# Up stores from ScalarE and GpSimd, rows of the last projection by GpSimd's queue, its sums in the third product, and the combination's gate columns two ahead

## The chip, the cores and the metric

The kernel runs on one core of a Trainium2 chip. The core has five engines that run side by side, each through its own list of instructions in order: TensorE (PE, matrix products), VectorE (DVE), ScalarE (ACT), GpSimd (POOL) and SyncE (SP). An engine that waits for a semaphore holds back all that stands behind in its list. Transfers between the memory outside (HBM) and the on-chip memory are issued by an engine and carried by 16 DMA engines. The metric is the device time of one execution in microseconds (us); the time before is the median of three runs.

## The reference

One decoder layer over 1024 positions of width 1024, in float32. The input x is normalised and projected by w_in into the columns of two branches and two gates. The branches are mixed, and a gated feed-forward network with a short causal convolution follows:

```python
y_a = conformer_branch(u_glu, ...)
y_b = ssd_branch(z, xbc, dt_raw, ...)
mix = (sigmoid(gate_a) * y_a + sigmoid(gate_b) * y_b) @ w_o
h = layer_norm(DN_ALPHA * h + mix, ln1_g, ln1_b)
u = causal_dwconv(h @ w_up, dw_w, dw_b)          # 3 taps, 2 x 2816 columns
gate, val = split(u, 2)
h = layer_norm(DN_ALPHA * h + (silu(gate) * val) @ w_down, ln2_g, ln2_b)
```

## The kernel before, in words

**Numbers in two parts.** Every product is made to float32's precision from three passes: a value is split into a high half (a cast by ScalarE, L731, L1006) and a low half (value less high half, by VectorE, L732, L1007), and `mm3` (L166 to L168) adds high x high, high x low and low x high. A weight tile is thus loaded by a transfer issued by SyncE, cast by ScalarE and subtracted by VectorE before TensorE can use it.

**Stages.** The sequence is handled in two halves of 512 positions up to the mixing; per half the layer norm, the branches (`mixers`), and `combine`. `combine(hh, hT, yT)` makes eight column tiles: for each j a product with the gate weights gb_j over hT, a sigmoid into the tile gb, a product with the branch's output weights sp_j over yT, and sum and product with gb. yT is the transposed state-space branch; its last quarter comes in just ahead of this stage: TensorE transposes it (L192), ScalarE writes the high half (L198), VectorE the low half (L199).

**The up projection** uses a scheme with seven block products instead of eight (Strassen's, in Winograd's form). The weights of a column pair j come as two 512 KB tiles, ra (blocks a11, a12) and rb (a21, a22). For the first LEAD = 8 columns two of the seven products are made early, in `up_first`, while the mixing's last norms are still running; their sums are stored to first_scr (L815, 16 stores of 256 KB) and loaded again in `up_rest` (L859, L860). `up_weights` makes s3 = a11 + a21, a21 + a22 and two more sums in place (L828 to L831) and splits three weights from them: w_s24 (from ra), w_s10 (from rb) and w_s3. Loads of ra take the ring "st" (three buffers, shared with all other weights), loads of rb the ring "raw" (three buffers). `up_rest` runs over j = 0 to 21: the products into the columns ug (gate) and uv (value), then for each the convolution of three taps (L883 on ScalarE, L887 twice on VectorE) into a buffer fo, of which there are three, then silu and the product (L898). An even j gives an early block that is stored at once (L908, b11); an odd j gives b2 (L910) and with it the sums t32 and t41 for the down projection (L912 to L915, stores L916 and L917). The first two columns of ug and uv are zeroed by GpSimd for each j (L846, L847).

**The down projection** (`down`) uses the same scheme with seven products p over 11 steps k. `load(p, k)` loads a block of the stored activations into the right half of a buffer dr and a weight block into its left half, forms the weight's sum where one is needed, and splits both in one go. Product 0 needs a11, product 1 a12, product 2 the sum a22 + a21 + a11, and product 3 the sum a11 + a21 (here called c3), product 6 c4 = a12 + a22 + a11 + a21. Before the change c3[k] is summed in product 0 (a21 loaded to c3[k] by L971, a11 added by L940), c4[k] begun in product 1 (L975) and completed in product 3. The raw buffers of these loads alternate between "st" and "raw". The eight residual rows (512 KB each, L936) are loaded when `down` begins.

**What sets the order.** The program is written by a scheduler that sorts instructions by the place in the code and by the priority of a `tc.high_priority(offset=...)` block; each engine then runs its list in order. All transfers before the change are issued by SyncE, so a transfer that waits for its data holds back every later one. A buffer of a ring is taken again when its last reader has finished, a store's end included.

## Time and profile before

| | |
|---|---|
| times of three runs | 2043.0, 2043.06, 2047.3 us (median 2043.06) |
| profiled execution | 2043.0 us, its span 2043.0 us |
| mean granted TensorE clock | 0.99 |
| busy: TensorE, VectorE, ScalarE, GpSimd | 1977.0, 1717.1, 1001.3, 146.8 us |
| moved | 275.10 MB, 135 GB/s in the mean |
| matmuls in a full window of 50 us | 222 |

In the rows below, the parts of a line of the timeline are its start, its duration, the engine and line number, the operation with output and input names (numbers left out), and in brackets the idle time of the engine ahead of it with what ended it. PE stands for TensorE's matmuls, PEld for its weight loads, SPq for SyncE's issues of transfers. Where TensorE has stood still, the granted clock drops to 0.5 and matmuls are 0.43 us apart instead of 0.23. A matmul's duration (about 0.39 us) is longer than its distance to the next, since they overlap.

### The profile page before, as it was taken

What the parts mean: (1) busy time and instruction counts of PE and PEld (TensorE: products, weight loads), DVE (VectorE), ACT (ScalarE), POOL (GpSimd) and SP (SyncE); (2) the same over time, 40 slices, a digit from 0 to 9 for tenths busy, and PEclk for the clock granted to TensorE, in tenths of its full rate; (3) what the DMA queues carried; (4) which work ended last, traced back from release to release, by engine and by line L of the source; (5) the groups of instructions that cost most, each with busy time, mean ns of one, the idle gap of its engine ahead of it and who ended that gap; (6) DMA issues with size and microseconds to landing.
All of it is one profiled execution on the core that took longest, in us unless ns stands there. A gap on an engine that the chain in (4) does not pass through costs nothing. (4 is left out here: it accounts for less than half of the span.)

```text
span 2043.0 us, 24683 instructions
## 1 busy us (share of the span) xinstructions
PE 1977.0 (97%) x9164; PEld 1627.7 (80%) x9164; DVE 1717.1 (84%) x2279; ACT 1001.3 (49%) x1431; POOL 146.8 (7%) x125
## 2 busy tenths in 40 slices
PE   7999999999999999999999999997899999989998
PEld 6888887888788888888888888876678888768886
DVE  7599999989766859999998976596888788789668
ACT  4465654556452356665454645453334445444432
POOL 2010101000400001010100040010000000000000
PEclk9999999999999999999999999998989999999999
DMA  6212223223436522222323253564343223287463
GB/s 218 93 68 89 87 93 103 98 103 114 160 124 218 200 93 73 93 78 87 117 88 109 107 175 127 207 234 174 124 138 119 95 98 117 101 316 267 145 226 109
DMA packets 99192, 275.10 MB, mean 135 GB/s; under 512 B 11264, under 2 KB 11264, under 8 KB 99072
## 3 DMA queue, kind: packets, MB, share of 16 engines
q1 hardware_dynamic: 99072, 273.52, 38.4%
q8 instruction: 72, 1.18, 0.2%
q14 instruction: 48, 0.39, 0.1%
HBM read 223.93 MB, written 49.55 MB: 134 GB/s over the span
## 5 line engine op out<-in xcount | busy, mean ns | idle before, releaser
L420 DVE SCALAR_TENSOR_TENSOR c<-v,pc,c 128x512 f32<-128x512 f32 x480 | 374.5, 803 | 7.7 <-ACT c L409 6.4
L478 POOL TENSOR_TENSOR au<-seg_mv,head_of 128x1024 fp32r<-128x1024 f32 x32 | 76.4, 2386 | 963.0 <-PE sm L487 730.1
L166 PE MATMUL acc<-hT,w_c 128*128 128x512 f32 x352 | 141.0, 401 | 0.0
L167 PE MATMUL acc<-hT,w_c 128*128 128x512 f32 x352 | 140.6, 399 | 0.0
L168 PE MATMUL acc<-hT,w_c 128*128 128x512 f32 x352 | 138.4, 393 | 0.0
L375 DVE SCALAR_TENSOR_TENSOR xbc<-u,pc,xbc 128x512 f32<-128x512 f32 x144 | 109.6, 773 | 0.7 <-ACT xbc L373 0.5
L1006 ACT CAST w_dn<-dr 128x1024 fp32r<-128x1024 f32 (+1 forms) x73 | 68.3, 944 | 76.6 <-PE sm L168 27.4
L167 PE MATMUL acc<-w_z,hT 128*128 128x512 f32 x256 | 100.8, 394 | 0.0
L166 PE MATMUL acc<-w_z,hT 128*128 128x512 f32 x256 | 100.8, 401 | 0.0
L168 PE MATMUL acc<-w_z,hT 128*128 128x512 f32 x256 | 100.7, 396 | 0.0
L154 ACT CAST w_c<-st_c 128x1024 fp32r<-128x1024 f32 x50 | 52.6, 1051 | 86.9 <-PE acc L168 66.2
L1007 DVE TENSOR_TENSOR w_dn<-dr,w_dn 128x1024 fp32r<-128x1024 f32 (+1 forms) x73 | 78.6, 1086 | 9.3 <-ACT w_dn L1006 9.1
L167 PEld LDWEIGHTS acc<-hT,w_c 128*128 128x128 f32 x352 | 66.1, 188 | 16.9 <-issue 3.8
L168 PEld LDWEIGHTS acc<-hT,w_c 128*128 128x128 f32 x352 | 66.1, 188 | 16.1 <-issue 2.6
L166 PEld LDWEIGHTS acc<-hT,w_c 128*128 128x128 f32 x352 | 66.1, 188 | 16.0 <-issue 2.6
L155 DVE TENSOR_TENSOR w_c<-st_c,w_c 128x1024 fp32r<-128x1024 f32 x47 | 60.5, 1287 | 20.3 <-ACT w_c L154 20.3
L166 PE MATMUL acc<-h1b,w_ue 128*128 128x512 f32 x176 | 68.8, 391 | 2.6 <-ACT w_ue L731 1.4
L731 ACT CAST w_s<-rb 128x1024 fp32r<-128x1024 f32 x22 | 23.2, 1053 | 94.7 <-PE sm L168 73.1
L166 PE MATMUL sm<-h1b,w_s 128*128 128x512 f32 x176 | 69.4, 395 | 0.0
L167 PE MATMUL sm<-h1b,w_s 128*128 128x512 f32 x176 | 69.2, 393 | 0.0
L168 PE MATMUL sm<-h1b,w_s 128*128 128x512 f32 x176 | 69.0, 392 | 0.0
L167 PE MATMUL acc<-h1b,w_ue 128*128 128x512 f32 x176 | 68.5, 389 | 0.0
(348 smaller groups left out, 5859.7 us busy)
## 6 DMA issues: line engine op xcount, KB each, us to landing
st_c<-wcol SPq DMA_DIRECT2D x50, 512.0 KB, 3.5
st_z<-wz SPq DMA_DIRECT2D x32, 512.0 KB, 3.5
dr<-wdown SPq DMA_DIRECT2D x55, 256.0 KB, 4.4
st_wo<-wo SPq DMA_DIRECT2D x24, 512.0 KB, 4.1
ra<-wup SPq DMA_DIRECT2D x22, 512.0 KB, 3.5
rb<-wup SPq DMA_DIRECT2D x22, 512.0 KB, 3.5
t_scr<-fo SPq DMA_DIRECT2D x22, 512.0 KB, 4.3
dr<-t_scr SPq DMA_DIRECT2D x44, 256.0 KB, 3.2
```

What stands on the lines that cost most here:

```text
L154: A.copy(w[:, 0, :], st)
L155: (eng or V).tensor_tensor(out=w[:, 1, :], in0=st, in1=w[:, 0, :].bitcast(F32), op=ALU.subtract)
L166: TE.matmul(ps, wa(0), xa(0), start=start, stop=False, skip_group_check=more)
L167: TE.matmul(ps, wa(0), xa(1), start=False, stop=False, skip_group_check=more)
L168: TE.matmul(ps, wa(1), xa(0), start=False, stop=stop, skip_group_check=more)
L375: V.scalar_tensor_tensor(out=o, in0=u[:, k : k + HALF], scalar=pc[:, wc + k : wc + k + 1], in1=o, op0=ALU.mult, op1=ALU.add,)
L420: V.scalar_tensor_tensor(out=accs[i], in0=v[:, k : k + HALF], scalar=pc[:, wc + k : wc + k + 1], in1=accs[i], op0=ALU.mult, op1=ALU.add,)
L478: G.tensor_tensor(out=au, in0=seg_mv[:, c, :].unsqueeze(1).to_broadcast([P, 8, P]), in1=head_of[:, g, :].unsqueeze(2).to_broadcast([P, 8, P]),
L731: A.copy(w[:, 0, :], src)
L1006: A.copy(w[:, 0, cs], src)
L1007: V.tensor_tensor(out=w[:, 1, cs], in0=src, in1=w[:, 0, cs].bitcast(F32), op=ALU.subtract)
```

## The change

1. In `combine` the product of gate column j is made two columns ahead: gates 0 and 1 stand ahead of the loop, and gate j + 1 is made in pass j from 1 to 6. The ring "gate" has three buffers instead of two.
2. In `up_first` ScalarE issues the 16 stores itself.
3. In `up_weights` the tile rb of column 0 takes a buffer of the ring "st", not of "raw".
4. In `up_rest` ug and uv are three fixed tiles u0 to u2 used in turn, zeroed once; the 44 memsets go. The stores b11, b2, t32 and t41 are issued by GpSimd.
5. In `down` GpSimd issues the loads of the rows; in the code they come after step 2 of products 0 and 2. c3[k] no longer takes a sum in product 0: for k < 5 a second copy of a11 is loaded to c3[k] by GpSimd, for k >= 5 a11 is loaded to c3[k] alone and split from there; a12 goes straight to c4[k] in product 1. Product 2 loads a21 and a22 and makes all three sums; product 3 makes none.

The diff, cut to its core:

```diff
+            def gate(j):
                 pg = bank(1)
                 project(pg, weights(wcol[CT_GB + j], f"gb{hh}_{j}"), hT)
-                gb = pl.tile([P, HALF], F32, tag="gate", bufs=2, name=f"gb{hh}_{j}")
+                gb = pl.tile([P, HALF], F32, tag="gate", bufs=3, name=f"gb{hh}_{j}")
                 A.activation(out=gb, in_=pg, func=AF.Sigmoid)
+                gates[j] = gb
+
+            gate(0)
+            gate(1)
+            for j in range(8):
+                if 0 < j < 7:
+                    gate(j + 1)
+                gb = gates[j]
...
-            SY.dma_start(first_scr[j][q], f)
+            A.dma_start(first_scr[j][q], f)
...
-            r2 = upp.tile([P, D], F32, tag="raw", bufs=3, name=f"rb{j}")
+            if j:
+                r2 = upp.tile([P, D], F32, tag="raw", bufs=3, name=f"rb{j}")
+            else:
+                r2 = wst.tile([P, D], F32, tag="st", name=f"rb{j}")
...
-        ug, uv = (
-            upp.tile([P, T + 32], F32, tag="u", bufs=3, name=f"f{n}{j}") for n in ("ug", "uv")
-        )
+        ug, uv = us[2 * j % 3], us[(2 * j + 1) % 3]
...
-        G.memset(ug[:, :2], 0.0)
-        G.memset(uv[:, :2], 0.0)
...
-            SY.dma_start(b11_scr[j], ov[:, early])
+            G.dma_start(b11_scr[j], ov[:, early])
...
-        SY.dma_start(b2_scr[j - NK], ov)
+        G.dma_start(b2_scr[j - NK], ov)
...
-        SY.dma_start(t32_scr[j - NK], t)
-        SY.dma_start(t41_scr[j - NK], a)
+        G.dma_start(t32_scr[j - NK], t)
+        G.dma_start(t41_scr[j - NK], a)
...
-        for t in range(8):
-            SY.dma_start(rs[t], h1_scr[t * P : (t + 1) * P, :])
+        def load_rows(ts):
+            for t in ts:
+                G.dma_start(rs[t], h1_scr[t * P : (t + 1) * P, :])
...
-                if p == 0:
+                if p == 0 and k < EARLY:
                     SY.dma_start(w_st, a11)
-                    SY.dma_start(c3[k], a21)
-                    add(c3[k], c3[k], w_st)
+                    G.dma_start(c3[k], a11)
+                elif p == 0:
+                    w_st = c3[k]
+                    SY.dma_start(w_st, a11)
                 elif p == 1:
+                    w_st = c4[k]
                     SY.dma_start(w_st, a12)
-                    SY.dma_start(c4[k], a22)
+                elif p == 2:
+                    other = raw("do")[:, E]
+                    SY.dma_start(other, a21)
+                    SY.dma_start(w_st, a22)
+                    add(c3[k], c3[k], other)
+                    add(w_st, w_st, c3[k])
                     add(c4[k], c4[k], w_st)
-                elif p == 2:
-                    SY.dma_start(w_st, a22)
-                    add(w_st, w_st, c3[k])
                 elif p == 3:
                     w_st = c3[k]
-                    add(c4[k], c4[k], c3[k])
...
+                if k == 2 and p in (0, 2):
+                    load_rows(range(2 * p, 2 * p + 4))
```

**How the order moves.** SyncE's list before, from the last stores of `up_first` on; first0_7 is the tile of the first block product of column 7, ra2 and rb0 are weight tiles of columns 2 and 0:

```order
L815 DMA first_scr5_131<-first0_5_11106 128x512
L822 DMA ra2_11414<-wup 128x1024
L815 DMA first_scr5_131<-first1_5_11121 128x512
L815 DMA first_scr6_132<-first0_6_11142 128x512
L815 DMA first_scr6_132<-first1_6_11157 128x512
L815 DMA first_scr7_133<-first0_7_11178 128x512
L815 DMA first_scr7_133<-first1_7_11193 128x512
L824 DMA rb0_11202<-wup 128x1024
L824 DMA rb1_11306<-wup 128x1024
L824 DMA rb2_11416<-wup 128x1024
```

The same place of SyncE's list after the change:

```order
L152 DMA st_ue7_11160<-wup 128x1024
L779 DMA h1_scr_125<-r7_10454 128x1024
L831 DMA ra0_11206<-wup 128x1024
L836 DMA rb0_11208<-wup 128x1024
L831 DMA ra1_11306<-wup 128x1024
L836 DMA rb1_11308<-wup 128x1024
L836 DMA rb2_11414<-wup 128x1024
```

The stores are gone from this list, rb0 stands right behind ra0, and ra2 has gone back behind the loads of columns 0 and 1. ScalarE's list after the change at the end of `up_first` (before, the DMA rows are not there):

```order
L823 COPY first1_6_11157<-acc507_11129 128x512
L823 COPY first0_7_11178<-acc508_11165 128x512
L824 DMA first_scr6_132<-first1_6_11157 128x512
L824 DMA first_scr7_133<-first0_7_11178 128x512
L823 COPY first1_7_11193<-acc508_11165 128x512
L824 DMA first_scr7_133<-first1_7_11193 128x512
L740 CAST w_s3_0_11221<-s3_0_11210 128x512
```

ScalarE now issues the last store between its last copy and the first cast of the up stage, w_s3_0.

VectorE's list before, at the first long gap of the up stage; fo1 and fo23 are the convolution buffers of column 2, fuv3 is the value tile of column 3, s4 the running sum of column 4:

```order
L887 SCALAR_TENSOR_TENSOR fo1_11507<-fug2_11432,pc_107,fo1_11507 128x1024
L887 SCALAR_TENSOR_TENSOR fo23_11511<-fuv2_11433,pc_107,fo23_11511 128x1024
L863 TENSOR_TENSOR s4_11648<-s4_11648,sm523_11655 128x512
L869 TENSOR_TENSOR fuv3_11537<-s3_11538,sm518_11541 128x512
L887 SCALAR_TENSOR_TENSOR fo23_11511<-fuv2_11433,pc_107,fo23_11511 128x1024
```

The same place after the change, where u1 and u2 take the place of fuv3 and fuv2:

```order
L895 SCALAR_TENSOR_TENSOR fo1_11501<-u1_11201,pc_107,fo1_11501 128x1024
L871 TENSOR_TENSOR s4_11636<-s4_11636,sm523_11641 128x512
L895 SCALAR_TENSOR_TENSOR fo23_11505<-u2_11202,pc_107,fo23_11505 128x1024
L877 TENSOR_TENSOR u1_11201<-s3_11530,sm518_11531 128x512
L895 SCALAR_TENSOR_TENSOR fo23_11505<-u2_11202,pc_107,fo23_11505 128x1024
```

The sum on s4 has moved ahead of the first tap of fo23; the sum into u1 (before: fuv3) stands behind that tap in both. One column later, the subtractions L921 and L922 on fo23 and fo12 (before: L913 and L914) stand ahead of the low half of w_s24_6, where before they stood behind it.

SyncE's list before, at the start of the last projection; c3 and c4 are the weight sums, dr the buffers of one step:

```order
L936 DMA rows_13949<-h1_scr_125 128x1024
L968 DMA dr_5_14057<-b11_scr4_138 128x512
L970 DMA dr_5_14057<-wdown 128x512
L975 DMA c4_0_13950<-wdown 128x512
...
L971 DMA c3_13948<-wdown 128x512 x11
L975 DMA c4_6_13956<-wdown 128x512
...
L908 DMA b11_scr10_144<-fo32_13788 128x512
...
L968 DMA dr_7_14097<-b11_scr6_140 128x512
L970 DMA dr_7_14097<-wdown 128x512
```

GpSimd's list after the change, its end (all that SyncE no longer issues there):

```order
L916 DMA b11_scr9_143<-fo31_13450 128x512
L982 DMA c3_13866<-wdown 128x512 x5
L918 DMA b2_scr9_154<-fo42_13577 128x1024
L924 DMA t32_scr9_165<-fo20_13573 128x1024
L925 DMA t41_scr9_176<-fo31_13450 128x1024
L916 DMA b11_scr10_144<-fo32_13710 128x512
L946 DMA rows_13867<-h1_scr_125 128x1024 x8
L918 DMA b2_scr10_155<-fo43_13837 128x1024
L924 DMA t32_scr10_166<-fo21_13833 128x1024
L925 DMA t41_scr10_177<-fo32_13710 128x1024
```

The eleven loads into c3 in a row are gone from SyncE's list (six remain there, each a weight of product 0), and GpSimd issues the other five, then all eight rows loads at one place, between the last b11 store and the last b2, t32 and t41 stores.

More of the change, by code (lines that the diff above doesn't have):

```diff
@@ L590, in combine @@
         with pool(f"comb{hh}") as pl:
-            mb = []
-            for j in range(8):
+            mb, gates = [], {}
+            def gate(j):
                 pg = bank(1)
                 project(pg, weights(wcol[CT_GB + j], f"gb{hh}_{j}"), hT)
-                gb = pl.tile([P, HALF], F32, tag="gate", bufs=2, name=f"gb{hh}_{j}")
+                gb = pl.tile([P, HALF], F32, tag="gate", bufs=3, name=f"gb{hh}_{j}")
                 A.activation(out=gb, in_=pg, func=AF.Sigmoid)
+                gates[j] = gb
[5 more added lines that the diff above has]
+                gb = gates[j]
                 ya = pl.tile([P, HALF], F32, tag="yb", bufs=2, name=f"yb{hh}_{j}")
@@ L646, in combine @@
             for j in range(8):
-                ga = pl.tile([P, HALF], F32, tag="gate", bufs=2, name=f"gl{hh}_{j}")
+                ga = pl.tile([P, HALF], F32, tag="gate", bufs=3, name=f"gl{hh}_{j}")
                 SY.dma_start(ga, g_scr[hh][j])
@@ L835, in up_weights, with up_rest @@
         return ue, w24, w10, w3
-    def up_rest(upp, bl, j, before):
+    def up_rest(upp, us, bl, j, before):
         ue, w24, w10, w3 = up_weights(upp, j)
-        ug, uv = (
-            upp.tile([P, T + 32], F32, tag="u", bufs=3, name=f"f{n}{j}") for n in ("ug", "uv")
-        )
+        ug, uv = us[2 * j % 3], us[(2 * j + 1) % 3]
         s = upp.tile([P, HALF], F32, tag="s", bufs=2, name=f"s{j}")
-        G.memset(ug[:, :2], 0.0)
-        G.memset(uv[:, :2], 0.0)
         early, late = slice(2, 2 + HALF), slice(2 + HALF, 2 + T)
@@ L915, in up_rest @@
         V.tensor_tensor(out=a[:, early], in0=b[:, early], in1=t[:, late], op=ALU.add)
-        SY.dma_start(t32_scr[j - NK], t)
-        SY.dma_start(t41_scr[j - NK], a)
+        G.dma_start(t32_scr[j - NK], t)
+        G.dma_start(t41_scr[j - NK], a)
     def down(upp, dp, g, b):
-        LAST = 8
+        LAST, EARLY = 8, 5
         X, Y = [bank(1) for _ in range(4)], [bank(0) for _ in range(4)]
@@ L1105 @@
     upp = ctx.enter_context(pool("up"))
+    us = [upp.tile([P, T + 32], F32, name=f"u{i}") for i in range(3)]
+    for u in us:
+        G.memset(u[:, :2], 0.0)
     before = None
     for j in range(NF):
-        before = up_rest(upp, bl, j, before)
+        before = up_rest(upp, us, bl, j, before)
     ffn_stack.close()
```

## The prediction

> **What bounds the kernel now.** I read the page first, then the table by windows of 50 us, then TensorE's waits in the windows that fell short, then the chain and the timeline around each wait. The page says who is the bound and which queue carries the transfers:
>
> ```profile
> PE 1977.0 (97%) x9164; PEld 1627.7 (80%) x9164; DVE 1717.1 (84%) x2279; ACT 1001.3 (49%) x1431; POOL 146.8 (7%) x125
> q1 hardware_dynamic: 99072, 273.52, 38.4%
> ```
>
> TensorE is busy for 97% of the span, so a change that leaves its work alone can only win back places where it stands still or runs at a lower clock. GpSimd (POOL) is nearly free. The windows show where TensorE falls short; the columns are start and end, length, then busy time and instructions of each engine, granted clock, DMA share and GB/s:
>
> ```profile
> 500.00:550.00 50.00, 46.32 (x209) 37.59 (x208) 40.34 (x53) 21.91 (x30) 16.36 (x11) 0.97 0.47 158
> 1400.00:1450.00 50.00, 36.77 (x149) 28.89 (x150) 33.78 (x46) 14.49 (x17) 0.20 (x2) 0.90 0.38 137
> 1450.00:1500.00 50.00, 44.83 (x186) 36.35 (x185) 46.03 (x56) 18.14 (x18) 0.60 (x6) 0.93 0.41 137
> 1500.00:1550.00 50.00, 45.50 (x190) 37.07 (x189) 45.21 (x55) 18.76 (x19) 0.60 (x6) 0.93 0.40 143
> 1550.00:1600.00 50.00, 50.00 (x222) 41.41 (x221) 37.79 (x43) 22.93 (x27) 0.40 (x4) 1.00 0.28 100
> 1800.00:1850.00 50.00, 42.36 (x171) 33.46 (x171) 41.52 (x46) 22.18 (x24) 0.10 (x1) 0.93 1.04 386
> ```
>
> A full window holds 222 matmuls, one per 0.225 us. The next to last row is such a window; the three ahead of it lack 73, 36 and 32 matmuls (16.4, 8.1 and 7.2 us), the last lacks 51 (11.5 us), and the first 13 (2.9 us; more in truth, since 16 of its 209 are short transposes). Those 46 us are what this change can work on. TensorE's waits in 1390 to 1560 and in 1790 to 1860 (total, times, longest) name who is late:
>
> ```profile
> PE sm L166 <- DVE fuv L869: 12.3, 3, 5.2
> PE sm L166 <- ACT w_s L731: 10.6, 2, 10.0
> PE acc L166 <- ACT w_dn L1006: 4.4, 1, 4.4
> PE acc L167 <- DVE w_dn L1007: 2.5, 2, 1.3
> ```
>
> **Part 1, gate columns two ahead.** Rows of TensorE in the first combination, with two short windows behind them (TensorE's own busy time is the first number after the length):
>
> ```profile
> 520.97 0.50 PE L166 MATMUL acc<-yT,w_sp 128*128 128x512 f32 x1 [0.83 <-ACT yT L198]
> 524.55 0.50 PE L167 MATMUL acc<-yT,w_sp 128*128 128x512 f32 x1 [2.85 <-DVE yT L199]
> 525.00:527.00 2.00, 2.00 (x8) 1.59 (x7) 0.00 (x0) 0.00 (x0) 0.00 (x0) 0.71 0.92 327
> 527.00:529.00 2.00, 2.00 (x6) 1.56 (x5) 0.00 (x0) 0.43 (x1) 1.49 (x2) 0.50 0.97 306
> ```
>
> TensorE has transposed the last quarter of yT and then waits 0.83 + 2.85 = 3.7 us for its two halves, and the clock then drops for two windows, 2 x 0.29 + 2 x 0.5 = 1.6 us. In the new order twelve matmuls of the third gate column, which need only hT, stand between the transposes and the first use of the new yT: 12 x 0.225 = 2.7 us of cover. About 1 us of the idle time stays, and after so short a gap I expect no drop of the clock: 3.7 - 1.0 + 1.6 = 4.3; I take **-4** (0 to -5.3). The second combination shows no such wait, so it counts nothing.
>
> **Part 2, stores by ScalarE and rb0 in the other ring.** This is the long wait. Rows of several engines, in order of start (the bracket is the idle time before and who ended it):
>
> ```profile
> 1394.40 9.52 SPq L815 DMA_DIRECT2D first_scr<-first  x5
> 1402.99 0.59 ACT L814 COPY first<-acc 128x512 f32<-128x512 f32 x1 [3.15 <-issue]
> 1403.97 1.39 SPq L824 DMA_DIRECT2D rb<-wup  x3
> 1407.89 0.69 DVE L828 TENSOR_TENSOR s<-ra,rb 128x512 f32<-128x512 f32 x1 [14.57 <-DMA rb<-wup]
> 1411.08 0.68 DVE L831 TENSOR_TENSOR ra<-ra 128x512 f32<-128x512 f32 x1
> 1411.80 1.05 ACT L731 CAST w_s<-ra 128x1024 fp32r<-128x1024 f32 x1
> 1412.89 0.80 PE L166 MATMUL sm<-h1s,w_s 128*128 128x512 f32 x1 [9.99 <-ACT w_s L731]
> ```
>
> SyncE holds the three rb loads behind five stores that wait for ScalarE's copies; VectorE starts its sums only when rb0 lands at 1407.9, and TensorE idles 9.99 us. With the stores on ScalarE and rb0 in a "st" buffer, rb0 is issued right behind ra0 and is there long before. What is late next is ScalarE's own order: the cast of s3_0 stands behind the last copy (ends 1403.6) and now behind that copy's store. With one issue at some 0.3 us (the t_scr row below) the cast runs about 1404.0 to 1404.7. VectorE then has four operations ahead of the end of ra0 (low half of s3_0, ra0, s3_1, ra0), 4 x 0.6 to 0.68, so 1407.2 to 1407.4; the cast of ra0 takes 1.05 and TensorE starts near 1408.5 instead of 1412.9: **-4.4**. The other 15 stores cost ScalarE 15 x 0.3 = 5 us in a stage where it is half idle. If ScalarE's issues were dearer (1 us), the gain would be 3.7; if VectorE did the sums without waiting for the cast, 7. The remaining gap of 5.6 us still costs the clock.
>
> **Part 3, stores by GpSimd and tiles u0 to u2.** The chain through the next two long gaps, with the store that starts the second as SyncE's row and TensorE's row at its end:
>
> ```profile
> 1469.14 5.80 DMA t_scr<-fo
> 1475.02 1.16 ACT fo L883
> 1477.46 0.68 DVE s L863
> 1478.14 0.61 DVE fuv L869
> 1504.66 0.32 SPq L916 DMA_DIRECT2D t_scr<-fo  x1
> 1504.66 5.18 DMA t_scr<-fo
> 1509.93 1.16 ACT fo L883
> 1513.70 0.79 PE L166 MATMUL sm<-h1s,w_s 128*128 128x512 f32 x1 [4.50 <-DVE fuv L869]
> ```
>
> A convolution buffer fo is taken again when its store has landed; ScalarE's scaling waits for that, VectorE's taps wait for ScalarE, and in VectorE's queue the sums that let TensorE go on (s, fuv) stand behind the first tap. In the new order only the sum on s4 (0.6 us) moves ahead of that tap; the one that TensorE waits for, now on u1, still stands behind it: **-0.6** at the first gap (5.2 us, the longest of the three in the waits). At the second gap the subtractions ahead of the t32 store are no longer behind the low half of ra6 (1.1 us, by the like operations of the L1007 row in Part 4): **-1.1**. Against this stands the store's issue by GpSimd, once in each gap. No transfer in this trace is issued by GpSimd. Its nearest rows are SyncE's 0.32 us of issue and the 5.18 and 5.80 us to landing; I bound the difference by -1 (the store no longer shares SyncE's queue with loads) and +5 (landing twice as long), and take **+1** each, nearer the lower end because GpSimd is 93% idle and the transfer itself is the same. Together +0.3.
>
> The Trainium skill, page "DMA: Bandwidth & Descriptors", section "Issuing engines are not separate DMA queues", says that another issuing engine saves issue time only; by that rule Part 2's store move would be worth next to nothing. The 9.52 us row speaks otherwise here: what is saved is the wait in order ahead of the loads, not the 0.3 us of an issue. The 44 memsets that go count nothing: none of TensorE's waits above names GpSimd.
>
> **Part 4, the last projection.** Rows of SyncE, TensorE and ScalarE at the change of stage, two windows behind the stall (there of TensorE alone: busy time, clock, DMA share, GB/s), and the page's row of VectorE's low halves (busy us, mean ns of one):
>
> ```profile
> 1813.31 3.59 SPq L975 DMA_DIRECT2D c<-wdown  x6
> 1817.29 7.04 SPq L971 DMA_DIRECT2D c<-wdown  x11
> 1836.69 1.04 ACT L1006 CAST w_dn<-dr 128x1024 fp32r<-128x1024 f32 x1 [7.13 <-DMA dr<-wdown]
> 1837.79 2.07 PE L166 MATMUL acc<-w_dn 128*128 128x512 f32 x4 [4.38 <-ACT w_dn L1006]
> 1837.00:1840.00 3.00, 2.21 (x5) 0.50 1.03 354
> 1840.00:1843.00 3.00, 3.00 (x8) 0.50 1.04 399
> L1007 DVE TENSOR_TENSOR w_dn<-dr,w_dn 128x1024 fp32r<-128x1024 f32 (+1 forms) x73 | 78.6, 1086 | 9.3 <-ACT w_dn L1006 9.1
> ```
>
> The DMA engines are full here (share 1.04 in the window above). SyncE issues 17 c loads in a row, the next dr is late by 7.13 us at ScalarE, and TensorE idles 4.38 us and then runs at half clock to 1843, 5.2 x 0.5 = 2.6 us more. The change halves this demand: products one and two now load 27 + 22 quarter-megabyte pieces instead of 33 + 33. Those 17 x 0.262 MB are 4.5 MB, at 386 GB/s 11.5 us of transfer, against a lateness of 4.4 us at TensorE. The rows (8 x 0.524 MB = 4.2 MB, 10.9 us) leave SyncE's queue ahead of the c loads and come from GpSimd's queue during the first product, so they still share the engines. Net the demand ahead of the stall falls: -4.4 - 2.6 = **-7**. The two waits for VectorE's low half (2.5 us) stand behind the last convolutions, which stay; I leave them. Bounds: 0 if the rows' transfers push dr_9 to dr_11 as late as now, -9.5 if those two waits go as well.
>
> The third product gets three sums per step instead of one, 22 operations of 0.6 us more; VectorE then needs 3 x 0.61 + 1.09 = 2.92 us a step, TensorE 12 x 0.225 = 2.7, so 11 steps fall back 2.4 us. Weight tiles made ahead (six buffers, 16 us) cover this: 0, and +2.4 without the cover.
>
> **Sum.** -4 - 4.4 + 0.3 - 7 = -15.1, on a profiled span of 2043.0 us, equal within 0.1 us to the median of the runs (2043.06): 2027.9.
>
> **Rivals.** *More than the sum:* rb0's early arrival gives VectorE ten microseconds' lead, and the gaps at 1478 and 1513 (5.2 and 4.5 us; with the clock at 0.93 over each window, 0.07 x 50 = 3.5 us behind each) close as well. For it: VectorE is busy 46.0 and 45.2 of 50 in those two windows, near its limit, where a lead counts. Against: the chain there goes through a store's landing, not through VectorE's amount of work. It would add 5.2 + 4.5 + 7 = 16.7 us: 2011.
>
> *Given back:* with VectorE at 92% of the windows, the 4.4 us of Part 2 come back as a longer gap at 1478, and the last projection stays bound by the full DMA engines (share 1.04), since the rows' 4.2 MB now fall into its first steps. Left: Part 1 and little else, 2038.
>
> *Slower, stores that land late from GpSimd's queue:* the fo buffer is freed later. The rows of a quiet column give the slack:
>
> ```profile
> 1569.65 0.32 SPq L917 DMA_DIRECT2D t_scr<-fo  x1
> 1577.05 1.14 ACT L883 ACTIVATE fo<-fuv,pc 128x1024 f32<-128x1024 f32 x1
> ```
>
> 1577.05 - 1569.65 - 5.2 = 2.2 us. A landing later by less than that costs only at the two gaps above. At 5 us later the two gaps pay 10 and seven later pairs 2.8 each, 30 us in all, of which 2 are in the sum: 2028 + 28 = 2056; at 3.5 us, 7 + 9 - 2 = 14, and the gain is used up. It decides from some 3.5 us. The Trainium skill, page "SBUF — State Buffer", section "SBUF: two separate sides" (its box on the trap of VectorE blocking transfers), says that GpSimd writes the descriptors of its transfers itself and is locked out while VectorE runs in a fast two-port mode: a transfer of 620 ns took 3100. No run here shows it yet, and VectorE's operations in this stage (0.68 us for 512 columns of two float32 operands) do not look like a fast mode; hence a small chance.
>
> *The change does not do what it says:* the last stores of the up stage (b2, t32, t41 of the last pair) stand in GpSimd's queue behind the eight rows loads, which wait for buffers and for one another. The second product needs b2 of the last pair in its last step, 13 or more steps of 2.7 us behind the row at 1837.8, so from about 1873. If the store lands later, TensorE waits there: 5 to 8 us back, 2034.
>
> **How the numbers follow.** Chances: forecast 0.60, more 0.12, given back 0.13, late stores 0.09, late queue 0.06. A measurement of this kernel can tell about 0.2%, 4 us, from no change. Faster by more: all of the first two, half of "given back", most of the last: 0.83. Same: the other half and a little of the late stores, 0.09. Slower: 0.08. The range reaches to 2010 for the larger gain and to 2042 for what is given back; outside lie the late stores and the extremes.
>
> **What would show it.** Right: rb0 issued before 1395 and TensorE starting the up columns near 1408 with a gap of 5 to 6 us; matmuls in 500 to 550 at 220 or more; the wait of 4.38 us for w_dn gone and no half clock behind 1837; t_scr stores landing within 6 us of their issue. Wrong: ScalarE waiting longer than now for t_scr, in each pair, or a wait for a dr load in the second product, or a first gap of 9 us or more.

## The result, and the profile after

| | before | changed |
|---|---|---|
| median of 4 runs each, us | 2043.39 | 2034.98 (2030.26 to 2037.27) |
| profiled run, and its span, us | 2043.06, 2043.0 | 2035.35, 2033.6 |

The ratio is 0.9951, with a 95% interval of 0.9937 to 0.9965: faster by 7 to 13 us. The forecast was 2027.9; 8.4 us of the 15.1 forecast came. The page after, engines and DMA queues (packets, MB, share):

```profile
PE 1978.0 (97%) x9164; PEld 1628.0 (80%) x9164; DVE 1710.7 (84%) x2285; ACT 1001.8 (49%) x1448; POOL 171.9 (8%) x141
q1 hardware_dynamic: 87696, 242.06, 35.9%
q0 software_dynamic: 7184, 25.69, 3.3%
q10 hardware_dynamic: 2304, 4.20, 0.6%
```

SyncE's queue is q1; the two new queues, GpSimd's q0 and ScalarE's q10, carry 25.7 and 4.2 MB that it carried before. The same windows as before:

```profile
500.00:550.00 50.00, 48.58 (x227) 39.71 (x226) 40.30 (x54) 22.98 (x31) 15.91 (x11) 1.00 0.48 168
1400.00:1450.00 50.00, 42.86 (x172) 33.70 (x171) 40.00 (x51) 18.98 (x20) 0.73 (x1) 0.93 0.40 135
1450.00:1500.00 50.00, 45.39 (x185) 36.39 (x184) 46.84 (x59) 16.77 (x17) 3.74 (x7) 0.93 0.45 160
1500.00:1550.00 50.00, 48.36 (x212) 39.39 (x211) 47.80 (x57) 22.02 (x24) 2.69 (x5) 1.00 0.35 121
1800.00:1850.00 50.00, 43.18 (x172) 34.53 (x173) 38.16 (x49) 24.03 (x36) 6.40 (x12) 0.90 0.80 295
```

TensorE's counts went from 209, 149, 186, 190, 171 to 227, 172, 185, 212, 172. Three windows gained about 20 matmuls each. The last gained nothing, although its DMA share fell from 1.04 to 0.80: the transfers are fewer and TensorE waits as long. Its waits in 1390 to 1560, then in 1790 to 1860 (total, times, longest):

```profile
PE sm L166 <- DVE u L877: 7.0, 3, 3.9
PE sm L166 <- ACT w_s L740: 6.0, 2, 5.3
...
PE acc L166 <- ACT u L875: 5.4, 1, 5.4
PE acc L166 <- ACT w_dn L1021: 1.8, 1, 1.8
```

The two waits of the up stage fell from 12.3 to 7.0 and from 10.6 to 6.0 us. At the change of stage the wait of 4.4 us for w_dn is down to 1.8, and a new one of 5.4 us stands ahead of it, for a copy of u by ScalarE. Rows around it, of SyncE, GpSimd, ScalarE and TensorE, and a short window of TensorE alone:

```profile
1785.96 3.08 SPq L985 DMA_DIRECT2D c<-wdown  x6
1786.23 2.71 POOL L982 DMA_DIRECT2D c<-wdown  x5 [17.06 <-PE acc L168]
1788.93 0.54 POOL L918 DMA_DIRECT2D b_scr<-fo  x1
1790.21 0.54 POOL L924 DMA_DIRECT2D t_scr<-fo  x1 [0.74 <-issue]
1798.77 1.15 ACT L891 ACTIVATE fo<-u,pc 128x1024 f32<-128x1024 f32 x1 [4.06 <-DMA b_scr<-fo]
1801.51 1.15 ACT L891 ACTIVATE fo<-u,pc 128x1024 f32<-128x1024 f32 x1 [1.59 <-DMA t_scr<-fo]
1804.27 0.79 PE L166 MATMUL acc<-h1s,w_s 128*128 128x512 f32 x1 [5.39 <-ACT u L875]
1811.90 4.25 POOL L946 DMA_DIRECT2D rows<-h_scr  x8 [3.97 <-PE sm L168]
...
1804.00:1808.00 4.00, 3.73 (x9) 0.54 0.01 2
```

Read it from the top. GpSimd's five c3 loads (L982) become free together and run ahead of the next-to-last pair's stores in GpSimd's list. The b2 store follows 2.7 us later, the t32 store behind it. ScalarE can scale into fo only when those stores have landed: it waits 4.06 and 1.59 us, and its copy of u, for which TensorE waits, stands behind both scalings. TensorE idles 5.39 us and restarts at a clock of 0.54: 9 matmuls in 3.73 us where 0.225 us each would give 16.6, another 1.7 us. The clock also falls behind the wait of 1.84 us for w_dn at 1837: it is 0.57 from 1838 to 1841, so that sign of the prediction (no half clock there) did not come.

### The profile page after: what moved, and what is told of

It is laid out like the page before. It is cut to its first block, busy times and chain, and to the rows that moved or that the text cites. A ratio compares the mean times of both kernels' runs of the same rounds, so it can differ in the third digit from the quotient of the medians.

```text
span 2033.6 us, 24571 instructions
## 1 busy us (share of the span) xinstructions
PE 1978.0 (97%) x9164; PEld 1628.0 (80%) x9164; DVE 1710.7 (84%) x2285; ACT 1001.8 (49%) x1448; POOL 171.9 (8%) x141
## 4 chain that ended last, share of the span: by engine, by line
PE 66%; DVE 24%; DMA 4%; issue 4%; ACT 1%; SPq 0%; DVEq 0%; ACTq 0%
PE acc L166 17%; PE acc L168 17%; PE acc L167 17%; DVE c L420 8%; PE sm L166 3%; PE sm L167 3%; PE sm L168 3%; DVE xbc L375 2%; DMA dr<-b_scr 1%; PE acc L357 1%; PE sm L534 1%; DVE fo L895 1%; DMA st_wo<-wo 1%; PE sm L515 1%; DVE w_so L155 1%
## 5 line engine op out<-in xcount | busy, mean ns | idle before, releaser
L166 PE MATMUL acc<-hT,w_c 128*128 128x512 f32 x352 | 141.1, 401 | 0.0
L895 DVE SCALAR_TENSOR_TENSOR fo<-u,pc,fo 128x1024 f32<-128x1024 f32 x88 | 111.5, 1279 | 8.5 <-ACT fo L891 7.8
L166 PE MATMUL acc<-w_z,hT 128*128 128x512 f32 x256 | 100.9, 401 | 0.0
L1021 ACT CAST w_dn<-dr 128x1024 fp32r<-128x1024 f32 (+1 forms) x73 | 60.8, 842 | 77.7 <-DVE dr L951 31.5
L1022 DVE TENSOR_TENSOR w_dn<-dr,w_dn 128x1024 fp32r<-128x1024 f32 (+1 forms) x73 | 69.6, 963 | 17.6 <-ACT w_dn L1021 17.5
L166 PEld LDWEIGHTS acc<-hT,w_c 128*128 128x128 f32 x352 | 66.1, 188 | 15.9 <-issue 2.6
L166 PE MATMUL acc<-h1s,w_s 128*128 128x512 f32 x168 | 66.6, 397 | 5.7 <-ACT u L875 5.7
L166 PE MATMUL acc<-h1b,w_ue 128*128 128x512 f32 x176 | 68.9, 392 | 2.6 <-ACT w_ue L740 1.4
L166 PE MATMUL sm<-h1b,w_s 128*128 128x512 f32 x176 | 70.3, 400 | 0.0
```

What stands on the lines that cost most here:

```text
L166: TE.matmul(ps, wa(0), xa(0), start=start, stop=False, skip_group_check=more)
L895: V.scalar_tensor_tensor(out=o, in0=u[:, k : k + T], scalar=pc[:, wc + k : wc + k + 1], in1=o, op0=ALU.mult, op1=ALU.add,)
L1021: A.copy(w[:, 0, cs], src)
L1022: V.tensor_tensor(out=w[:, 1, cs], in0=src, in1=w[:, 0, cs].bitcast(F32), op=ALU.subtract)
```

## The experiments

The theories. Part 4's gain was lost because the c3 copies in GpSimd's queue delay the stores behind them (the queue theory), or too many bytes come at once at the change of stage, whoever issues them (the bytes theory), or the rows share the engines with the products' loads (the rows theory). For Part 3, which gave more than forecast: VectorE's order moved with the issuing engine (the order theory), or GpSimd's queue lands stores differently (the landing theory). Each ratio is against before on the same chip, where its median was 2044.4 to 2045.6. The change itself was timed beside a before of 2043.39, so a difference between its median and one below carries 1 to 2 us of doubt. "Up" is the distance in the trace from the first product with w_ue to the last, "down" from there to the last with w_dn: before 439.9 and 234.6 us, after 431.8 and 235.4. Among the profiled runs with the change's combination the first product with w_ue starts anywhere from 1348.5 to 1354.1 us, so these distances, and not the totals, carry the verdicts by stage.

**c3 copies by SyncE (e1).**

```diff
-                    G.dma_start(c3[k], a11)
+                    SY.dma_start(c3[k], a11)
```

> The changed kernel, but the five early copies of a11 into c3 are issued by SyncE instead of GpSimd, at the same point. Question: why do the stores of the last odd column but one (b2, t32, t41) land 9.7 to 12.6 us after their issue, so that ScalarE waits for fo and TensorE idles 5.39 us at 1804. Theory A, the DMA engines are full: eleven c3 loads (2.9 MB) start at 1786 and share the 16 engines with the stores; who issues them does not matter. Then the landing stays at 9 us or more, the gap at 4 to 6 us, the time within 2 us of the changed kernel's 2035. Theory B, GpSimd's own list and queue: the stores stand behind the five loads. Then the stores land in 3 to 5 us, the gap falls under 1 us and the time to 2026 to 2029.

Measured: 2026.88 (2024.03 to 2027.84), ratio 0.9905 (0.989 to 0.992), 8.1 us below the change by the medians; up 432.0, down 228.9. GpSimd and TensorE at the same place:

```profile
1785.21 0.53 POOL L918 DMA_DIRECT2D b_scr<-fo  x1 [17.11 <-DVE fo L906]
1798.93 0.50 PE L166 MATMUL acc<-h1s,w_s 128*128 128x512 f32 x1 [1.15 <-ACT u L875]
1831.24 0.50 PE L166 MATMUL acc<-w_dn 128*128 128x512 f32 x1 [1.73 <-ACT w_dn L1021]
```

b2 is stored as soon as its taps are done, and the 5.39 us become 1.15. All eleven c loads still run at once, so bytes alone, whoever issues them, are not what cost those 5 us.

**c3 copies by ScalarE.**

```diff
-                    G.dma_start(c3[k], a11)
+                    A.dma_start(c3[k], a11)
```

> The changed kernel with the five early c3 copies issued by ScalarE, side by side with SyncE's six. GpSimd's list is as in e1, the burst as in the changed kernel: eleven loads from two engines within about 3 us. Theory B (place in GpSimd's list): b2 is issued at once, the stores land as in e1 (7 to 8 us), gap at 1804 of about 1 us, time 2026 to 2028. Theory A', the burst comes too fast (two issuers put 2.9 MB ahead of t32 and t41, one issuer 1.8 MB): the stores land after 9 us or more, gap of 4 to 5 us, time 2033 to 2036. ScalarE itself loses 5 x 0.3 us ahead of two casts, under 1 us for TensorE.

Measured: 2026.81 (2025.68 to 2028.56), ratio 0.9917 (0.99 to 0.9933); down 231.5. The same gain from a third engine: what matters is that the loads leave GpSimd's queue. The issues of 1783 to 1800 (median us to landing) separate its list from its transfers, first after the change, then here:

```profile
c<-wdown SPq DMA_DIRECT2D x6, 256.0 KB, 6.5
c<-wdown POOLq DMA_DIRECT2D x5, 256.0 KB, 7.1
t_scr<-fo POOLq DMA_DIRECT2D x2, 512.0 KB, 11.9
b_scr<-fo POOLq DMA_DIRECT2D x1, 512.0 KB, 9.7
```

```profile
c<-wdown SPq DMA_DIRECT2D x6, 256.0 KB, 8.4
c<-wdown ACTq DMA_DIRECT2D x5, 256.0 KB, 9.7
t_scr<-fo POOLq DMA_DIRECT2D x2, 512.0 KB, 8.3
b_scr<-fo POOLq DMA_DIRECT2D x1, 512.0 KB, 7.6
```

Behind five loads in its own queue, a store takes 9.7 to 11.9 us from issue to landing; with the same loads in another queue 7.6 to 8.3, and the loads are what gets slower. So the stores lost both ways: 2.7 us in the list and 2 to 4 us in the transfers. The amount moved is the same: 4.47 MB in the 14.04 us from the first of these loads after the change, 4.50 MB here. ScalarE pays for it: its five issues took 5.11 us, where 1.5 were expected, TensorE waits 0.90 and 0.53 us for what stands behind them, and the down distance is 2.6 us longer than with the copies by SyncE.

**c3 copies spread out.** Only the first copy stays at the change of stage; the others' a11 are loaded again in the third product.

```diff
-        LAST, EARLY = 8, 5
+        LAST, EARLY = 8, 11
...
-                    G.dma_start(c3[k], a11)
+                    if k == 0:
+                        G.dma_start(c3[k], a11)
...
-                    add(c3[k], c3[k], other)
+                    if 0 < k < EARLY:
+                        first = raw("do")[:, E]
+                        SY.dma_start(first, a11)
+                    else:
+                        first = c3[k]
+                    add(c3[k], first, other)
```

> The changed kernel, but a11 comes through the ring of raw buffers in product 0 for all eleven steps, and a second time through the ring in product 2, where c3 = a11 + a21 is written; only one load goes to c3 early, so that the buffers are handed out as before. The burst at 1786 is 1 load instead of 11; product 2 loads 10 pieces more (4 x 0.262 MB in 2.7 us, 386 GB/s, near what the engines carried in 1800 to 1850). Theory A and theory B: the gap at 1804 goes (5.4 us and about 3 us of clock), stores land in 3 to 5 us; time 2027, up to 2031 if product 2 is starved. Rival C, the stores are late because GpSimd issues them at all: landing stays over 9 us, time 2033 or more.

Measured: 2031.97 (2028.91 to 2035.01), ratio 0.9932 (0.9915 to 0.9949); down 235.8. The gap ahead of the copy of u is 0.84 us, as the queue theory has it, but the loads come back later. TensorE's waits for w_dn from 1790 to the end:

```profile
PE acc L167 <- DVE w_dn L1028: 3.4, 3, 1.9
PE acc L166 <- ACT w_dn L1027: 2.6, 1, 2.6
```

After the change TensorE has no wait behind 1860. Here VectorE is late three times from 1887 to 1897, in the third product. Spreading takes the stall away and pays there.

**The last projection as before.** The whole of down() is undone (rows, c3 copies, sums); Parts 1 to 3 stay.

```diff
-        LAST, EARLY = 8, 5
+        LAST = 8
...
-        def load_rows(ts):
-            for t in ts:
-                G.dma_start(rs[t], h1_scr[t * P : (t + 1) * P, :])
+        for t in range(8):
+            SY.dma_start(rs[t], h1_scr[t * P : (t + 1) * P, :])
...
-                if p == 0 and k < EARLY:
+                if p == 0:
                     SY.dma_start(w_st, a11)
-                    G.dma_start(c3[k], a11)
+                    SY.dma_start(c3[k], a21)
+                    add(c3[k], c3[k], w_st)
...
-                if k == 2 and p in (0, 2):
-                    load_rows(range(2 * p, 2 * p + 4))
```

> The changed kernel with the last projection as it was before (rows and c3, c4 loads by SyncE, sums in products 0, 1 and 3); the up stores stay with GpSimd. The prediction gave this part 7 us: then 2042. The reading of the two traces: from the first to the last matmul of the up and down stages the part gave nothing net (the distance from the last w_ue product to the last w_dn product is 234.6 us before and 235.4 after), because the new gap at 1804 took what the old one at 1837 gave back: then 2033 to 2036, with the gap at 1837 back and none at 1804.

Measured: 2030.56 (2028.29 to 2032.72), ratio 0.9925 (0.991 to 0.994): 4.4 us faster than with Part 4 by the medians, though the intervals of the two ratios just touch. Up 430.0, down 233.8, so 1.6 us of it lie in the down distance. TensorE's waits in 1780 to 1850:

```profile
PE acc L166 <- ACT w_dn L1014: 6.8, 1, 6.8
PE acc L166 <- ACT u L875: 0.7, 1, 0.7
```

The old wait is there in full (6.8 us; 4.4 before) and the new one is not. As written, Part 4 trades one for the other and loses. This run also speaks against the bytes theory: the eight rows loads stand in SyncE's list at the same time, 7.04 MB are moved from 1780 to 1800, and GpSimd's b2 lands after 7.4 us, t32 and t41 after 7.7 (median), with no c3 load ahead of them in their queue.

**Up stores by SyncE (e4).** All 44 stores of b11, b2, t32 and t41.

```diff
-            G.dma_start(b11_scr[j], ov[:, early])
+            SY.dma_start(b11_scr[j], ov[:, early])
...
-        G.dma_start(b2_scr[j - NK], ov)
+        SY.dma_start(b2_scr[j - NK], ov)
...
-        G.dma_start(t32_scr[j - NK], t)
-        G.dma_start(t41_scr[j - NK], a)
+        SY.dma_start(t32_scr[j - NK], t)
+        SY.dma_start(t41_scr[j - NK], a)
```

> The changed kernel with the 44 stores b11, b2, t32 and t41 issued by SyncE again; c3 and rows loads stay with GpSimd. The prediction counted +1 us at each of two gaps for GpSimd's issue and landing: then 2 us less in the up stage, up stage gaps (waits for u, L877) of 5 us instead of 7. Rival: the up stage gained 8.1 us where 4.1 were forecast because the stores left SyncE's list, where loads stood behind them: then 3 to 5 us more in the up stage, gaps of 9 to 12 us as before. For the gap at 1804: theory A keeps it.

Measured: 2034.18 (2032.26 to 2037.09), ratio 0.9942 (0.9923 to 0.996), the same in total and not by stage: up 435.8, 4.0 us longer, down 233.5, 1.9 us shorter. Medians from issue to landing, over 11 stores each: b2 2.9 us by GpSimd and 2.6 by SyncE, t32 3.6 and 3.1, t41 4.8 and 4.0. GpSimd's land 0.3 to 0.8 us later and TensorE's gaps are nevertheless shorter, so the landing theory does not explain the gain. At the change of stage the gap is 5.4 us here too: the b2 store now stands behind SyncE's six c3 loads (issue 1788.39, 2.77 us; the store at 1791.26). That is the queue theory again, in the other list.

**One kind of store each.** b11 and b2 by SyncE, t32 and t41 by GpSimd:

```diff
-            G.dma_start(b11_scr[j], ov[:, early])
+            SY.dma_start(b11_scr[j], ov[:, early])
...
-        G.dma_start(b2_scr[j - NK], ov)
+        SY.dma_start(b2_scr[j - NK], ov)
```

> The changed kernel with the stores b11 and b2 (22) issued by SyncE, t32 and t41 by GpSimd. What made the up stage 4 us shorter with the stores at GpSimd (distance from the first to the last w_ue product: 431.8 us, e4 435.8). Theory L, SyncE's list: b11 and b2 wait longest for VectorE at the head of that list in e4 (33 us in all) and hold the loads behind them: then this kernel has 435 to 436 us and gaps for u of 10 us. Theory O, VectorE's order: with t32 and t41 at GpSimd the scheduler puts the sum on s4 ahead of the first tap of fo23 and the low sum of u2 ahead of fo24's tap, and it does so here too: 432 us, gaps of 7 us.

and t32 and t41 by SyncE, b11 and b2 by GpSimd:

```diff
-        G.dma_start(t32_scr[j - NK], t)
-        G.dma_start(t41_scr[j - NK], a)
+        SY.dma_start(t32_scr[j - NK], t)
+        SY.dma_start(t41_scr[j - NK], a)
```

> The changed kernel with t32 and t41 (22 stores) issued by SyncE, b11 and b2 by GpSimd. VectorE's order in the up stage is that of e4. Theory O: 435 to 436 us from the first to the last w_ue product, gaps for u of 10 us. Theory L: between the two, 432 to 433 us, since the stores that wait longest have left SyncE's list.

Measured: 2032.12 (2031.18 to 2035.2), ratio 0.9936 (0.992 to 0.9952), up 431.0; and 2037.16 (2036.16 to 2039.06), ratio 0.9961 (0.9947 to 0.9975), up 435.1. VectorE ahead of the sum u that TensorE waits for, at the second long gap, with TensorE's row; first with t32 and t41 on GpSimd, then on SyncE:

```profile
1494.05 3.79 DVE L895 SCALAR_TENSOR_TENSOR fo<-u,pc,fo 128x1024 f32<-128x1024 f32 x3
...
1498.96 0.68 DVE L877 TENSOR_TENSOR u<-s,sm 128x512 f32<-128x512 f32 x1
...
1499.70 0.50 PE L166 MATMUL sm<-h1s,w_s 128*128 128x512 f32 x1 [1.70 <-DVE u L877]
```

```profile
1492.81 1.28 DVE L895 SCALAR_TENSOR_TENSOR fo<-u,pc,fo 128x1024 f32<-128x1024 f32 x1
1495.10 2.48 DVE L895 SCALAR_TENSOR_TENSOR fo<-u,pc,fo 128x1024 f32<-128x1024 f32 x2 [1.00 <-ACT fo L891]
...
1498.10 1.28 DVE L895 SCALAR_TENSOR_TENSOR fo<-u,pc,fo 128x1024 f32<-128x1024 f32 x1
...
1499.89 0.68 DVE L877 TENSOR_TENSOR u<-s,sm 128x512 f32<-128x512 f32 x1
...
1500.62 0.50 PE L166 MATMUL sm<-h1s,w_s 128*128 128x512 f32 x1 [4.19 <-DVE u L877]
```

With t32 and t41 on GpSimd three taps stand ahead of u; on SyncE there are four, and one of them waits 1.00 us for a scaling. From the first tap to u that is 4.9 us against 7.1, and TensorE's gap is 1.70 against 4.19. The change itself has the first order (1.64), the kernel with all stores on SyncE the second (3.93). This is what the order theory says. In these four kernels order and queue change together for t32 and t41; the landings above speak against the queue, and the kernel with the gates as before, below, has the queue of the change with another order. Something besides the order is left at the first long gap with all stores on SyncE: there VectorE waits 1.24 us for rb, and the gap is 5.21 us against 4.60 with only t32 and t41 on SyncE.

At the change of stage these two kernels have the longest gaps of all ahead of the copy of u, 9.01 and 7.95 us. In the first, b2 stands in SyncE's list behind six c3 loads and lands after 12.9 us; in the second, t32 and t41 do and land after 11.6. That is the queue theory once more; down is 236.7 and 237.9.

**The store of the first products back on SyncE, and rb0 back in its ring.**

```diff
-            A.dma_start(first_scr[j][q], f)
+            SY.dma_start(first_scr[j][q], f)
...
-            if j:
-                r2 = upp.tile([P, D], F32, tag="raw", bufs=3, name=f"rb{j}")
-            else:
-                r2 = wst.tile([P, D], F32, tag="st", name=f"rb{j}")
+            r2 = upp.tile([P, D], F32, tag="raw", bufs=3, name=f"rb{j}")
```

> The changed kernel with the first stores issued by SyncE and rb0 in the raw ring again. Prediction's Part 2: 4.4 us slower (2039.5), the first up gap 10 us instead of 5.3. Rival: the early rb0 also gives VectorE its lead, and the later gaps grow too: 8 us slower (2043), gaps for u of 11 to 12 us instead of 7.

Measured: 2040.2 (2037.43 to 2045.07, 11 runs), ratio 0.9983 (0.9974 to 0.9992), 5.2 us above the change; up 435.6. The wait for w_s has its old size, 9.94 us.

**Only rb0 back in its ring** (the second half of that diff).

> The changed kernel with only rb0 back in the raw ring, the first stores still by ScalarE. If the wait in SyncE's list was the whole of Part 2, as the prediction says, this is as fast as the changed kernel (2035), first gap 5 to 6 us: rb0 has a free raw buffer once the stage of the blocks has ended. If the ring matters (the raw ring belongs to a pool whose memory is free only when the early columns' tiles are), the gap is 8 to 10 us and the time 2039.

Measured: 2036.31 (2033.87 to 2038.66, 5 runs), ratio 0.9961 (0.9947 to 0.9974); up 433.4. The first gap is 5.33 us, as with the whole part (5.30): the store move alone makes it. The other buffer shortens the next gap from 3.07 to 1.44 us. The total's 1.3 us lies within its uncertainty.

**Gates as before.** The loop of combine() and its two "gate" buffers are those of before.

```diff
-            gate(0)
-            gate(1)
...
-                if 0 < j < 7:
-                    gate(j + 1)
-                gb = gates[j]
```

> The changed kernel with the combination as before (gate column j in pass j). Prediction's Part 1: 4 us slower than the changed kernel (2039), with the waits of 0.8 and 2.85 us for yT back and the clock below 1 in 500 to 550. Rival: the 3.2 us that the traces differ by at the next stage are lost again later, since the w_o product there waits for the norms anyway (0.7 us were lost by the start of the up stage): then 2 to 2.5 us.

Measured: 2041.87 (2037.93 to 2045.42, 11 runs), ratio 0.9990 (0.9979 to 1.0001), 6.9 us above the change. The two old waits for yT are back, 0.83 and 2.86 us, and the window from 500 holds 208 matmuls for 227. That is some 4 us, and the up stage starts 3.7 us later than in the change. The rest lies in gaps of code that this edit leaves alone: 4.23 us for 1.64 in the up stage (up 434.9), 3.75 for 1.84 behind 1840. The second is inside the 1.6 to 3.8 us that the kernels with the same `down` show. The first comes from VectorE's order, which moved here too. Rows of VectorE, SyncE, GpSimd and TensorE (L732, L822, L915 and L166 are here the low half, the load of ra, the t32 store and TensorE's product):

```profile
1496.60 1.22 DVE L732 TENSOR_TENSOR w_s<-ra,w_s 128x1024 fp32r<-128x1024 f32 x1
1497.84 0.33 SPq L822 DMA_DIRECT2D ra<-wup  x1
1499.56 0.53 POOL L915 DMA_DIRECT2D t_scr<-fo  x1 [5.58 <-DVE fo L913]
1508.91 0.50 PE L166 MATMUL sm<-h1s,w_s 128*128 128x512 f32 x1 [4.23 <-DVE u L868]
```

All 44 stores are GpSimd's, as in the change, but the low half of w_s24 stands ahead of the t32 store's subtractions again, as before the change. The store is then issued behind the load of ra and lands after 6.2 us; in the change it is issued ahead of that load and lands after 3.6. So the order alone, with the queue kept, brings the gap back. The kernel is thus not a clean undoing of Part 1.

**Rows really late.** c3 copies by SyncE, and rows 4 to 7 tied to the first product's end by a copy of one column, which the load then overwrites.

```diff
-                    G.dma_start(c3[k], a11)
+                    SY.dma_start(c3[k], a11)
...
-                if k == 2 and p in (0, 2):
-                    load_rows(range(2 * p, 2 * p + 4))
+                if k == 2 and p == 0:
+                    load_rows(range(4))
...
+                if p == 0:
+                    V.tensor_copy(rs[4 + t][:, :1], rs[t][:, :1])
+                    load_rows([4 + t])
```

> The kernel of e1 (c3 copies by SyncE), and the rows of the second half (4 of 8, 2.1 MB) are loaded only after product 0 has written the first half's rows (a copy of one column by VectorE makes each load wait). Question: what makes TensorE wait 1.76 and 1.73 us for dr at 1826 and 1831 in e1, where the DMA engines are full from 1808 to 1832. If it is the amount in flight: 2.1 MB less at 400 GB/s is 5 us, both gaps go and the time falls from 2027 to 2023 to 2024. If dr waits for the place of its store or for a buffer: gaps stay, time 2026 to 2028.

Measured: 2023.63 (2020.77 to 2026.72), ratio 0.9895 (0.9879 to 0.9912): the fastest version here, 20.7 us below before and by the medians 3.3 below the one with c3 by SyncE (the intervals overlap). Down 226.3, 2.6 us shorter than there. GpSimd's rows, then TensorE's only wait from 1780 to 1870, then the window:

```profile
1806.96 2.14 POOL L946 DMA_DIRECT2D rows<-h_scr  x4 [1.32 <-PE sm L168]
1838.45 0.54 POOL L946 DMA_DIRECT2D rows<-h_scr  x1 [11.05 <-DVE rows L1094]
...
PE acc L166 <- ACT u L875: 1.1, 1, 1.1
...
1800.00:1850.00 50.00, 49.06 (x215) 40.28 (x216) 40.76 (x59) 27.95 (x44) 6.44 (x12) 1.00 0.88 327
```

In the change the rows of the third product were issued with the others, all eight at 1811.9, because nothing made them wait; the place of the call in the code did not. Once the stores are free of the c3 copies, the rows are next in line: TensorE's 1.76 and 1.73 us for w_dn go with it, and 215 matmuls stand where 172 stood.

## Why the prediction was half right

**Part 1, right.** Forecast -4 with about 1 us of idle time left and no drop of the clock. After, TensorE's only wait there is

```profile
524.84 0.50 PE L167 MATMUL acc<-yT,w_sp 128*128 128x512 f32 x1 [1.42 <-DVE yT L199]
```

The window gained 18 matmuls, 18 x 0.225 = 4.05 us, and its clock is 1.00. At the start of the up stage the two traces differ by less, 2.5 us, within the spread of the traces ahead of it.

**Part 2, right in size and working.** Forecast a gap of 5.6 us. The rows:

```profile
1384.25 0.33 SPq L836 DMA_DIRECT2D rb<-wup  x1
1400.58 0.58 ACT L823 COPY first<-acc 128x512 f32<-128x512 f32 x1 [3.15 <-PE acc L168]
1401.19 0.33 ACTq L824 DMA_DIRECT2D first_scr<-first  x1
1401.56 0.62 ACT L740 CAST w_s<-s 128x512 fp32r<-128x512 f32 x1 [0.40 <-ACT first L823]
1404.74 1.04 ACT L740 CAST w_s<-ra 128x1024 fp32r<-128x1024 f32 x1
1405.84 0.79 PE L166 MATMUL sm<-h1s,w_s 128*128 128x512 f32 x1 [5.30 <-ACT w_s L740]
```

rb0 is issued early, the last copy and its store (0.33 us) come ahead of the cast, and the cast of ra0 sets the end. -4.7 in the gap, 5.2 by the median of the kernel without it. The page "DMA: Bandwidth & Descriptors" of the Trainium skill, section "Issuing engines are not separate DMA queues", by which the move would have saved only issue time, did not decide here: what went is rb0's wait in SyncE's order, behind the five stores, from which it was issued at 1403.97.

**Part 3, +0.3 forecast, -4.0 measured** (up 435.8 with the stores on SyncE, 431.8 without; the totals do not show it). At the first gap the working held: the sum on s4 ahead of one tap was priced at -0.6, and the two kernels with one kind of store each differ by 0.70 there (4.60, 3.90). The step that failed is the second gap. "the subtractions ahead of the t32 store are no longer behind the low half of ra6" was counted as their own -1.1, against +1 for the store. But the earlier store also goes out ahead of the load of ra. It landed after 3.6 us, where the chain shown in the prediction has 5.18, and VectorE then makes three taps in a row without a wait and u behind them. The gap fell by 2.86 us (4.50 to 1.64), and the clock of the window rose from 0.93 to 1.00. The price of +1 for the queue was of the right sign and near in size: issue 0.54 for 0.33 us, landing 0.3 to 0.8 us later in the medians.

**Part 4, -7 forecast, a loss measured** (down 235.4 against 234.6 before and 233.8 with down() undone; +4.4 by the median of that kernel). The step that failed: "products one and two now load 27 + 22 quarter-megabyte pieces". The c3 copies entered the sum as bytes and never as five instructions in GpSimd's list, ahead of the stores that I had moved there myself in Part 3. The old wait did shrink, 4.38 to 1.84 us. With the copies in another queue much of the forecast comes: the down distance is 5.7 us shorter than before with SyncE's, 3.1 with ScalarE's, and 8.3 with the rows really late. The sums of the third product cost nothing, as forecast: no wait of TensorE behind 1860.

The spans of the two profiled runs are 9.4 us apart: 2.5 us ahead of the up stage and 8.1 in it are gained, 0.8 in the last projection and 0.4 behind it are lost. The up stage gave 4.0 us more than forecast and the last projection 7.8 less. That these two misses partly cancel in the total is luck.

**The rivals.** "The change does not do what it says" had the mechanism, stores behind loads in GpSimd's queue, at 0.06. It named the eight rows, the last pair and the second product; it was the five c3 copies, the pair before and TensorE's next column, 70 us earlier. "Stores that land late" did not come: the medians over all pairs stay within 4.8 us. The lockout that the Trainium skill's page "SBUF — State Buffer", section "SBUF: two separate sides", describes is not seen: b2's median of 2.9 us by GpSimd is 0.3 above SyncE's. "More than the sum" was right that both later gaps shrink (5.17 to 3.88, 4.50 to 1.64), but not through rb0's lead: without Part 2 they are 3.91 and 1.84. "Given back" was right that the last projection gained nothing, and wrong in its reason: the DMA share fell from 1.04 to 0.80, and the gap at 1478 did not grow.

## What to carry to other kernels

For each transfer that a change moves, write down what now stands ahead of and behind it in its new queue, and who waits for those; bytes alone miss it. A load that waits for nothing is issued as soon as its buffer is free, wherever the code has it; to make it late, give it something real to wait for. Where a scheduler orders the engines, compare the waiting engine's order at every long gap after a change of queue, since it can move without a line of that engine's code being changed.

## What the runs showed of the hardware

A store of half a megabyte behind loads of a quarter megabyte in its own queue took 9.5 to 12.9 us from issue to landing: 9.7 and 11.9 behind five in GpSimd's queue (the change), 9.9 and 10.6 behind six in SyncE's (all stores by SyncE). With the same loads in another queue it took 7.6 and 8.3 us (ScalarE's) or 5.8 and 7.9 (SyncE's). The Trainium skill says in "DMA: Bandwidth & Descriptors", section "SWDGE vs HWDGE vs iDMA", that each DMA engine takes turns between internal queues and that GpSimd's feed others than SyncE's and ScalarE's; that agrees with these rows, while the section on issuing engines, read alone, would have the two landings equal. The t32 store at the second long gap landed after 3.5 to 4.4 us in the eleven kernels where it was issued ahead of the half-megabyte load of ra, and after 5.2 and 6.2 us in the two where it was issued behind it, by GpSimd and by SyncE alike. An issue by GpSimd took 0.53 to 0.54 us, by SyncE and ScalarE 0.33 when alone; in a row of c3 loads SyncE took 0.51 each after the change, and both took about 1.0 where SyncE and ScalarE issued side by side.

The granted clock does not fall at every stop. After gaps of 1.4 and 1.6 us it held (1.00), and after 2.67 us before the change too (1.00 from 1445 to 1454); after 1.84 us at 1837 it was 0.57 for 3 us. So the length of the gap alone does not decide. Behind 3.9 us it was 0.50 for 6 us, and behind 5.4 us 0.54 for the next 4.
